# Sums of weights inside DRAM in halves and from the filter stage on, one split for the gates' four sums, and the last projection's first block loaded at another time

## The chip, the cores and the metric

The kernel runs on one core of a Trainium2 chip. The engines named here are PE (TensorE, the matrix products), DVE (VectorE), ACT (ScalarE), POOL (GpSimd) and SP (SyncE, which here only issues transfers); PEld is PE's loading of weights. The metric is device time in microseconds (us) of one execution. The kernel before was timed in three runs: 2376.48, 2383.24 and 2383.48 us, median 2383.24.

## The reference

One encoder layer on two sequences (`x_prompt` and `x_sample`) of 1024 rows and 1024 channels, all in 32-bit floats. After a norm, one projection makes everything else; a Fourier branch and a Hyena branch (two long convolutions with computed filters) are gated, projected, mixed and projected once more:

```python
xn = rmsnorm(x, g_pre)
p = xn @ w_in                      # fv, fg, hv (3 parts), hg, mg (2 parts): 8 x 1024 columns
fz = fftn(fv in 4 groups, axes=(sequence, group channel)).real
y_f = (fz * silu(fg)) @ w_fourier_out
v, x1, x2 = split(short_conv(hv, w_short), 3)
kf = hyena_filters(...)            # rfft of a two-sided filter, two orders
z = v
for n, gate in enumerate((x1, x2)):
    z = gate * long_conv(z, kf[:, n], hyena_d[n])
y_h = (z * silu(hg)) @ w_hyena_out
g_f, g_h = split(sigmoid(mg + b_merge), 2)
out = (g_f * y_f + g_h * y_h) @ w_out
return x + rmsnorm(out, g_post)
```

## The kernel before

Each 32-bit operand of a product is split into a rounded high part and the rest (`split`, L170 for the cast on ACT and L180 for the subtraction on DVE or POOL), and a product is three matmuls of high and low parts (`mm`, L193). So most groups of the profile bear the lines L170, L180 and L193, and go by their tiles' names. A `T`, `we`, `wh`, `wl` or `oT` is such a part; a subtraction `wl<-wr,wh` makes a low part.

The program runs through these stages:

1. *The start* (`phase_fourier`): 128-row blocks of the first sequence are loaded (L328), normed and transposed (`tpx`), the transposed rows are stored to DRAM (`d_x<-xg`, L362), and sums `eo` of them meet weights made from `w_fv` (`wfv` loads, L385; `wes`, `we`, `wo`) in the products `pfv`.
2. *The filter stage* (`phase_main`, about 230 to 650 us): 16 iterations make the filters' spectra (`kt`, stored to `d_k`) and between them project gates of the first sequence (`spill_gate`, product `pin`, weights `wr` loaded by SP, their low parts `wl` made on POOL).
3. *The branches* (`branches`, L1034 to L1105): for each step one `front(i)`, its gates, and the way back. Here `k<-d_k` loads bring the filter spectra, and the first sequence's weight parts go out to DRAM by transfers on POOL's queue (`d_w<-wh`, `d_w<-wl`, L858).
4. *The gates' projections of the second sequence* (`phase_tail`): products of 1024 x 1024 matrices cut in quarters, by Strassen and Winograd in seven products. One operand's seven blocks are B11, B21, B22 and the sums T1 to T4. The rows of the second sequence come back from DRAM (`xraw`, L1513) in four steps k; each step makes four sums of 512 elements and splits each of them into its tile T2, T3, T1 or T4 (eight operations). The other operand's sums are made by `prepare` (`wraw`, `wsum`, `s1` to `s4`). In the same stretch `last_sums` makes the sums of the last projection's weights `w_out`: loads `ws` (L1244), three subtractions on POOL, stores `d_t` (L1250).
5. *The nets*: 112 product steps of four projections (Fourier and Hyena output weights for two sequences), whose second operands are sums of weights that are read from DRAM (`wl<-d_s`, L1305). What is loaded and rounded when is written in a table of due steps: `at(98, load_own, ...)` has the step 98 issue a load. The rooms `x0{}` and `x1{}` and the four sum tiles are shared with the nets' own blocks.
6. *The last projection*: `prepare("o", ...)` for its rows (`wraw<-d_m`), blocks B11, B21 and B22 from `d_wo` (`load_own`, L1396, tiles `oB`), sums T1 to T4 from `d_t` (`load_sum`, L1402, tiles `oT`), each rounded in place by `round_z`. `first` opens it with products 11 (with B11) and 12 (with B21), then `part2` takes `s2` with T2, and so on.

The sums in `d_s` are made by transfers from DRAM to DRAM, some of which add to what is there (`accum_op=ADD`). `weight_sums` lists them: 11 for each of the two weights, 1 MB each, all on POOL's queue. Some read or add to what an earlier one wrote, and so wait for it, for example

```python
load(3, v[1, 0])
more(3, v[1, 1])
```

`front(i)` issues two of them for i = 2 to 12 (L1132 plain ones, L1133 adding ones). Eight copies of `w_out` by 512 KB to `d_wo` (L1524) are on SP's queue; they depend on nothing.

The order of the instructions on every engine isn't that of the text: a planner places the whole program by its own costs, and only `issue_after` and the dependences bind it. Queues issue in order: what stands behind a waiting instruction waits too.

Of the kernel before, what the change touches and what calls it, by code (L numbers as in the profile page):

```python
# [160 lines left out]
class K:  # L161
# [824 lines left out]
    def phase_main(self, nct=8, nb=NB, nf=16):  # L986
        tc, nc, a = self.tc, self.nc, self.a
        with ExitStack() as es:
# [25 lines left out]
            rates = self.filter_rates(1, 0, ws)  # L1014
            for i in range(nf):
                nxt = self.filter_taps((i + 1) % 2, (i + 1) // 2, rates, ws) if i + 1 < nf else None
# [14 lines left out]
            self.sums_due = list(self.weight_sums())  # L1031
            self.branches(nb, nct, ws)

    def branches(self, nb, nct, ws):  # L1034
# [13 lines left out]
        def front(i):  # L1048
            with tc.issue_after(self.pooled.ins):
                for f in self.sums_due[max(2 * i - 4, 0):max(2 * i - 2, 0)]:  # L1050
                    f()
            b, n, c = steps[i]
            src = self.conv(1, c, ws, "v", b) if n == 0 else Z.pop(c)
            return self.conv_front(src, ws)
# [69 lines left out]

    def weight_sums(self):

        nc, a = self.nc, self.a
        out = []
        for n, w in enumerate(("w_fo", "w_ho")):
            v = a[w].rearrange("(j i) p (h c) -> i h p j c", i=2, h=2)  # L1130
            d = self.d_s[n]
            load = lambda p, src, d=d: out.append(lambda: nc.gpsimd.dma_start(d[p], src))  # L1132
            more = lambda p, src, d=d: out.append(lambda: nc.gpsimd.dma_start(d[p], src, accum_op=ADD))  # L1133
# [10 lines left out]
            more(4, v[0, 1])  # L1144
        return out

    def phase_tail(self):
# [10 lines left out]
        with ExitStack() as es:  # L1158
# [96 lines left out]
            ROOM = ["T2", "T3", "T1", "T4"]  # L1255
# [26 lines left out]
            def block(g, i):  # L1282
# [8 lines left out]
                if i == 0:  # L1291
                    blocks[g] = gs.tile([P, 2, 4, 512], F32R, tag=ROOM[(g - 1) % 4], name="n", bufs=1)
# [106 lines left out]
            def load_sum(nm):  # L1399
                t = Z[nm] = gs.tile([P, 2, 4, 512], F32R, tag=nm, name=f"o{nm}", bufs=1)  # L1400
# [10 lines left out]
            for nm, room, t in (("B21", "x1{}", 88), ("B11", "x0{}", 98), ("B22", "x1{}", 110)):  # L1411
                at(t, load_own, nm, room)
            at(100, load_sum, "T4")
            at(104, load_sum, "T2")
            at(108, load_sum, "T3")
            for k in range(4):
                at(92 + k, round_z, "B21", k)
                at(100 + k, round_z, "B11", k)
            for k in range(2):
                at(103 + k, round_z, "T4", k)  # L1420
                at(107 + k, round_z, "T2", k)
# [87 lines left out]
            T = {j: gs.tile([P, 2, 4, 512], F32R, tag=j, name=j, bufs=1) for j in order}  # L1509
            for k in range(4):  # L1510
# [6 lines left out]
                for j, q in zip(order, (3, 1, 0, 2)):  # L1517
                    self.split(T[j][:, 0, k], T[j][:, 1, k], r[:, q], "dve", "act")
            pairs = lambda z: [(t[:, 0], t[:, 1]) for t in z]
            quad = lambda t: [(t[:, 0, k], t[:, 1, k]) for k in range(4)]  # L1520
            for j in order:
# [175 lines left out]
```

## Time and profile before

| | us |
|---|---|
| median of three runs | 2383.24 |
| the profiled execution | 2382.25 |
| its span | 2380.5 |
| PE busy | 2330.1 (98%) |
| DVE busy | 1973.3 (83%) |
| ACT busy | 1115.5 (47%) |
| POOL busy | 430.7 (18%) |
| mean granted clock of PE | 0.994 |

In a row of waits stand the engine, line and tile that waited, what released it, the total in us, how many times, and the longest. In a row of a timeline stand start and length in us, engine, line, operation, out<-in, shape, how many, and in brackets the idle time before it and its releaser; "SPq" is SP's queue of transfers. In a table of stretches stand the stretch and its length, busy us (and instructions) of PE, PEld, DVE, ACT and POOL, the granted clock of PE, the mean share of time in which the 16 DMA engines are busy, and GB/s. In a group of operations of one tile stand the least, median and greatest length in ns, and the first and last start. In a group of the page stand busy time, mean ns of one, and idle time before them with its releasers.

### The profile page before, as it was taken

The numbers are of one execution on the slowest core, as the hardware profiler recorded it, in microseconds if no ns is written. First come the engines' busy times: TensorE is split into PE (matmuls) and PEld (weight loads), VectorE is DVE, ScalarE is ACT, GpSimd is POOL, SyncE is SP. The second block draws the span as 40 slices with busy tenths as digits, with TensorE's granted clock in tenths as the row PEclk, the third lists the DMA queues.
The fourth block names the chain that finished last, engine by engine and source line by source line (L and its number), as shares of the span: only waits on it lengthen the run. The fifth ranks groups of instructions, "written<-read, shape, count | busy, mean of one in ns | idle before, by whom it ended". The sixth has DMA issues, their size and how long they took to land.

```text
span 2380.5 us, 36106 instructions
## 1 busy us (share of the span) xinstructions
PE 2330.1 (98%) x12796; PEld 2022.8 (85%) x12796; DVE 1973.3 (83%) x3416; ACT 1115.5 (47%) x2083; POOL 430.7 (18%) x406
## 2 busy tenths in 40 slices
PE   6999999999999999999999999999999999999998
PEld 5999888888888888888889888888788888888786
DVE  7775688878889999999889999997765578778987
ACT  6555667776753333334222332323444365557443
POOL 2342322222243333221000000111300000101211
PEclk9999999999999999999999999999999999999999
DMA  9646655555578787745444444445754688988644
GB/s 318 207 148 220 189 175 166 166 178 171 176 261 272 244 251 231 222 149 195 153 147 133 133 142 144 140 142 177 264 186 161 217 267 272 262 310 258 174 160 142
DMA packets 241888, 471.31 MB, mean 198 GB/s; under 512 B 24103, under 2 KB 81801, under 8 KB 241387
## 3 DMA queue, kind: packets, MB, share of 16 engines
q1 hardware_dynamic: 217949, 398.06, 51.0%
q0 software_dynamic: 23536, 70.91, 10.4%
q8 instruction: 101, 1.65, 0.3%
q14 instruction: 81, 0.66, 0.1%
q10 hardware_dynamic: 221, 0.04, 0.0%
HBM read 322.63 MB, written 173.54 MB: 208 GB/s over the span
## 4 chain that ended last, share of the span: by engine, by line
PE 52%; DVE 3%; DMA 3%; issue 1%; ACT 0%; SPq 0%; DVEq 0%; POOL 0%; POOLq 0%; ACTq 0%
PE pin L193 17%; PE pg L193 14%; PE pn L193 10%; PE pT L193 5%; PE pX L193 5%; DMA d_m<-gt 1%; PE tph L904 1%; DMA xraw<-d_x 1%; DMA d_sh<-x 0%; DVE gt L180 0%; DMA g<-d_g 0%; DVE T L180 0%; DVE wl L180 0%; DVE xraw L180 0%; DVE r L180 0%
## 5 line engine op out<-in xcount | busy, mean ns | idle before, releaser
L193 PE MATMUL pin<-x,wh 128*128 128x512 f32 x2880 | 909.8, 391 | 2.5 <-ACT ktmp L794 2.4
L193 PEld LDWEIGHTS pin<-x,wh 128*128 128x128 f32 x2880 | 534.3, 188 | 103.4 <-ACT ktmp L794 2.6
L193 PE MATMUL pin<-x,wl 128*128 128x512 f32 x1440 | 563.2, 391 | 0.0
L180 POOL TENSOR_TENSOR wl<-wr,wh 128x512 fp32r<-128x512 f32 x132 | 224.2, 1699 | 1104.5 <-ACT wh L170 668.6
L193 PEld LDWEIGHTS pin<-x,wl 128*128 128x128 f32 x1440 | 271.0, 188 | 50.8
L193 PE MATMUL pn<-n,wh 128*128 128x512 f32 x896 | 276.4, 389 | 0.1
L193 PEld LDWEIGHTS pn<-n,wh 128*128 128x128 f32 x896 | 168.1, 188 | 35.8 <-DVE n L180 0.5
L193 PE MATMUL pn<-n,wl 128*128 128x512 f32 x448 | 174.6, 390 | 1.6 <-DVE wl L180 1.5
L180 DVE TENSOR_TENSOR t<-pX,k 128x1024 f32<-128x1024 f32 x128 | 155.4, 1214 | 8.7 <-DMA k<-d_k 5.9
L193 PE MATMUL pX<-bh,cfwd 128*128 128x256 f32 x768 | 162.4, 288 | 0.0
L193 PE MATMUL pT<-cinv,yh 128*128 128x256 f32 x768 | 146.0, 284 | 0.3 <-DVE T0s L180 0.3
L170 ACT CAST wh<-wr 128x512 fp32r<-128x512 f32 x132 | 81.6, 618 | 132.2 <-PE pin L193 90.3
L170 ACT CAST bh<-b 128x512 fp32r<-128x512 f32 x144 | 88.4, 619 | 99.3 <-DVE b L180 73.7
L193 PEld LDWEIGHTS pX<-bh,cfwd 128*128 128x128 f32 x768 | 126.4, 190 | 3.1 <-DVE t L180 0.4
L193 PEld LDWEIGHTS pT<-cinv,yh 128*128 128x128 f32 x768 | 122.6, 190 | 6.6 <-ACT sg L1080 0.7
L170 ACT CAST yh<-y 128x512 fp32r<-128x512 f32 x96 | 59.6, 620 | 144.5 <-DVE y L180 144.4
L1344 POOL DMA_DIRECT2D d_m<-gt x32 | 27.5, 861 | 471.7 <-DVE gt L180 442.1
L193 PE MATMUL pT<-cinv,yl 128*128 128x256 f32 x384 | 109.1, 284 | 0.7 <-DVE yl L180 0.6
L193 PE MATMUL pX<-bl,cfwd 128*128 128x256 f32 x384 | 109.2, 284 | 0.4 <-DVE bl L180 0.4
L180 DVE TENSOR_TENSOR bl<-b,bh 128x512 fp32r<-128x512 f32 x144 | 101.5, 709 | 0.5 <-ACT bh L170 0.5
L193 PEld LDWEIGHTS pn<-n,wl 128*128 128x128 f32 x448 | 84.1, 188 | 19.7 <-DVE wl L180 2.5
L180 DVE TENSOR_TENSOR y<-t 128x512 f32<-128x512 f32 x128 | 91.8, 717 | 5.4 <-PE pT L193 4.9
(370 smaller groups left out, 5045.8 us busy)
## 6 DMA issues: line engine op xcount, KB each, us to landing
k<-d_k SPq DMA_DIRECT2D x128, 512.0 KB, 4.1
wr<-in_w_in SPq DMA_DIRECT2D x132, 256.0 KB, 3.4
d_g<-gt SPq DMA_DIRECT2D x124, 256.0 KB, 2.7
wl<-d_s SPq DMA_DIRECT2D x56, 512.0 KB, 5.8
d_k<-kt SPq DMA_DIRECT2D x128, 128.0 KB, 2.2
d_k<-kt SPq DMA_DIRECT2D x64, 256.0 KB, 2.4
g<-d_g SPq DMA_DIRECT2D x64, 256.0 KB, 5.5
r<-d_g SPq DMA_DIRECT2D x60, 256.0 KB, 5.7
```

The source lines that it names most:

```text
L170: self.rounded = nc.scalar.copy(h, src)
L180: return e.tensor_tensor(out, a, b, op=op)
L193: return self.nc.tensor.matmul(out, lhsT, rhs, start=start, stop=stop, skip_group_check=shared)
L904: nc.tensor.transpose(tp[:, q * P:(q + 1) * P], eo[:, e, q], self.ident)
L1344: nc.gpsimd.dma_start(dst, t, accum_op=ADD)
```

## The change

- `weight_sums` cuts each of its 22 transfers into two halves of 512 KB (over the row blocks j), 44 in all, and appends the eight copies to `d_wo`, which thereby go to POOL's queue. The list of 52 is `self.due`.
- `transfers(2)` issues two of them in each filter iteration from the second on (15 times) and then two in each front until the list is empty.
- The gates' opening has one tile `rooms` for the four sums, and each step k splits all four sums in one operation of 2048 elements on ACT and one on DVE. The nets' blocks and the last projection's sums use the four parts of `rooms` where they had tiles T1 to T4.
- In the last projection B11 is loaded at step 60 into `x1{}` and rounded at 64 to 67 (before: loaded at 98 into `x0{}`, rounded at 100 to 103); B21 is loaded at 98 into `x0{}` and rounded at 101 to 104 (before: 88 into `x1{}`, 92 to 95). The sums are loaded in the order T2, T3, T1 at steps 100, 104, 108 (before T4, T2, T3), T2 is rounded at 105 and 106 and T3 at 109 and 110; after `first`, T4 is loaded and T1 rounded, then the preparation is finished, B22 and T4 rounded.

```diff
@@ phase_main
+            self.due = self.weight_sums()
             for i in range(nf):
+                if i:
+                    self.transfers(2)
...
-            self.sums_due = list(self.weight_sums())
             self.branches(nb, nct, ws)
@@ branches
         def front(i):
-            with tc.issue_after(self.pooled.ins):
-                for f in self.sums_due[max(2 * i - 4, 0):max(2 * i - 2, 0)]:
-                    f()
+            if i < 16:
+                self.transfers(2)
@@
+    def transfers(self, n):
+        with self.tc.issue_after(self.pooled.ins):
+            for f in self.due[:n]:
+                f()
+        self.due = self.due[n:]
+
     def weight_sums(self):
...
+        def put(d, src, **how):
+            for j in (slice(0, 2), slice(2, 4)):
+                out.append(lambda j=j: nc.gpsimd.dma_start(d[:, j], src[:, j], **how))
...
-            load = lambda p, src, d=d: out.append(lambda: nc.gpsimd.dma_start(d[p], src))
-            more = lambda p, src, d=d: out.append(lambda: nc.gpsimd.dma_start(d[p], src, accum_op=ADD))
+            load = lambda p, src, d=d: put(d[p], src)
+            more = lambda p, src, d=d: put(d[p], src, accum_op=ADD)
...
+        for k in range(8):
+            out.append(lambda k=k: nc.gpsimd.dma_start(self.d_wo[k], a["w_out"][k * P:(k + 1) * P]))
         return out
@@ phase_tail
-            ROOM = ["T2", "T3", "T1", "T4"]
+            ROOM = [3, 1, 0, 2]
...
-                    blocks[g] = gs.tile([P, 2, 4, 512], F32R, tag=ROOM[(g - 1) % 4], name="n", bufs=1)
+                    blocks[g] = rooms[:, ROOM[(g - 1) % 4]]
...
-                t = Z[nm] = gs.tile([P, 2, 4, 512], F32R, tag=nm, name=f"o{nm}", bufs=1)
+                t = Z[nm] = rooms[:, {"T2": 2, "T3": 3, "T1": 1, "T4": 0}[nm]]
...
-            for nm, room, t in (("B21", "x1{}", 88), ("B11", "x0{}", 98), ("B22", "x1{}", 110)):
+            for nm, room, t in (("B11", "x1{}", 60), ("B21", "x0{}", 98), ("B22", "x1{}", 110)):
                 at(t, load_own, nm, room)
-            at(100, load_sum, "T4")
-            at(104, load_sum, "T2")
-            at(108, load_sum, "T3")
+            at(100, load_sum, "T2")
+            at(104, load_sum, "T3")
+            at(108, load_sum, "T1")
             for k in range(4):
-                at(92 + k, round_z, "B21", k)
-                at(100 + k, round_z, "B11", k)
+                at(64 + k, round_z, "B11", k)
+                at(101 + k, round_z, "B21", k)
             for k in range(2):
-                at(103 + k, round_z, "T4", k)
-                at(107 + k, round_z, "T2", k)
+                at(105 + k, round_z, "T2", k)
+                at(109 + k, round_z, "T3", k)
...
-            T = {j: gs.tile([P, 2, 4, 512], F32R, tag=j, name=j, bufs=1) for j in order}
+            rooms = gs.tile([P, 4, 2, 4, 512], F32R, name="rooms")
...
-                for j, q in zip(order, (3, 1, 0, 2)):
-                    self.split(T[j][:, 0, k], T[j][:, 1, k], r[:, q], "dve", "act")
+                self.split(rooms[:, :, 0, k], rooms[:, :, 1, k], r, "dve", "act")
...
-            for j in order:
-                Y[j] = quad(T[j])
-            for k in range(8):
-                nc.sync.dma_start(self.d_wo[k], a["w_out"][k * P:(k + 1) * P])
+            for j, q in zip(order, (3, 1, 0, 2)):
+                Y[j] = quad(rooms[:, q])
...
-            for k in range(2):
-                round_z("T3", k)
-            load_sum("T1")
             with tc.issue_after(self.copied.ins):
-                list(prep)
+                load_sum("T4")
                 for k in range(2):
                     round_z("T1", k)
+                list(prep)
                 for k in range(4):
                     round_z("B22", k)
-            Y["T1"] = quad(Z["T1"])
+                for k in range(2):
+                    round_z("T4", k)
+            Y["T4"] = quad(Z["T4"])
```

## The prediction

> **What bounds the kernel now.** I read the page's first part, then TensorE's (PE's) waits over the whole span, then a table of stretches around the places where those waits lie, and last the order in time at each place.
>
> ```profile
> span 2380.5 us, 36106 instructions
> PE 2330.1 (98%) x12796; PEld 2022.8 (85%) x12796; DVE 1973.3 (83%) x3416; ACT 1115.5 (47%) x2083; POOL 430.7 (18%) x406
> ```
>
> ```profile
> PE tpx L359 <- DVE x L344: 11.0, 1, 11.0
> PE pfv L193 <- ACT we L170: 4.5, 3, 2.3
> PE pg L193 <- ACT m L1215: 3.7, 1, 3.7
> PE pg L193 <- DVE wl L180: 3.4, 1, 3.4
> PE pX L193 <- DVE b L180: 2.2, 2, 1.8
> PE pn L193 <- DVE wl L180: 1.5, 1, 1.5
> PE pg L193 <- ACT gt L885: 1.2, 1, 1.2
> ```
>
> ```profile
> 0.00:50.00 50.00, 27.94 (x130) 22.16 (x131) 33.74 (x75) 34.01 (x57) 10.16 (x23) 0.90 0.96 334
> 240.00:640.00 400.00, 400.00 (x2195) 348.55 (x2194) 325.96 (x739) 276.60 (x592) 98.00 (x60) 1.00 0.55 173
> 690.00:970.00 280.00, 276.38 (x1625) 243.24 (x1625) 260.20 (x403) 99.47 (x178) 101.06 (x116) 1.00 0.82 255
> 1686.00:1706.00 20.00, 15.10 (x53) 11.57 (x52) 15.89 (x20) 6.82 (x13) 8.37 (x6) 0.83 0.97 346
> 2200.00:2225.00 25.00, 20.07 (x80) 15.57 (x79) 23.38 (x32) 14.55 (x21) 6.55 (x8) 0.93 0.99 267
> ```
>
> TensorE is the bound: 2330.1 of 2380.5 us. The change touches no matmul, so all that it can win lies in the 50.4 us in which PE is idle, and in stretches where a wait is followed by a lower granted clock (the column before the last two of the table: DMA share and GB/s close each row). The table places it: 22.06 us idle in the first 50, none in the filter stage, 3.62 in the first branches, 4.90 where the gates' projections open, 4.93 where the last projection opens. The clock costs about 50 x 0.10 = 5.0, 20 x 0.17 = 3.4 and 25 x 0.07 = 1.8 us more in the first, fourth and fifth of these stretches.
>
> **The change, part by part.**
>
> *The copies of the output weights leave the start.* Before, SP issues eight copies of 512 KB inside DRAM to `d_wo`:
>
> ```profile
> 8.78 5.67 SPq L1524 DMA_DIRECT2D d_wo<-in_w_out  x6
> 16.53 1.91 SPq L385 DMA_DIRECT2D wfv<-in_w_fv  x2
> 19.59 2.28 SPq L1524 DMA_DIRECT2D d_wo<-in_w_out  x2
> ```
>
> ```profile
> 30.35 0.52 PE L193 MATMUL pfv<-we,eh 128*128 128x260 f32 x2 [1.95 <-ACT we L170]
> 40.82 0.50 PE L193 MATMUL pfv<-we,eh 128*128 128x260 f32 x2 [2.35 <-ACT we L170]
> ```
>
> 4.19 MB at the stretch's 334 GB/s is 12.6 us of transfer time, and the issues hold SP for 7.95 us, ahead of the Fourier weights `wfv`. The DMA share is 0.96: the transfers compete. In the changed order SP goes from the x rows straight to `wfv`, and ACT and DVE prepare the next weights earlier. The two waits shown are 4.3 us, all waits for ACT's `we` 4.5; the clock lost after them is up to 5.0. Bounds: a gain of 9 (4.5 and nearly all of the clock's loss), and a loss of 2, since DVE is busy 33.74 of 50 us here and splitting a weight early delays an `eo` behind it. The 11.0 us at the very start stay: the x rows already stand ahead of the copies. I take **-5**: the two waits and a little of the clock.
>
> *Sums of weights halved and spread.* Before, 22 transfers of 1 MB go out in the branches, two per front, and one that reads what the last one wrote stands close behind it on POOL's queue:
>
> ```profile
> POOL d_s L1133 <- DMA d_s<-d_s: 20.6, 3, 13.5
> ```
>
> ```profile
> 935.91 1.21 POOL L1133 DMA_DIRECT2D d_s<-in_w_ho  x1 [13.48 <-DMA d_s<-d_s]
> ```
>
> ```profile
> 932.90 1.22 DVE L180 TENSOR_TENSOR t<-pX,k 128x1024 f32<-128x1024 f32 x1 [3.42 <-DMA k<-d_k]
> ```
>
> Behind the blocked POOL queue stand the low parts `wl` and the spills `d_w` of the input weights; beside it `k` loads come late, DVE waits, and the 1.8 us wait of `pX` for `b` follows. All PE idle time of these branches is 3.62 us: that is the upper bound of the gain. Afterwards there are 44 half transfers and the 8 copies. 30 go out in the filter stage, two in each of 15 iterations, 22 in the first 11 fronts; a transfer that depends on another is an iteration (15 of them fill the 400 us of the second row: 27 us each) or a front behind it, longer than the 13.5 us of the longest wait. POOL pays 30 issues more at up to the 1.21 us of the row quoted, 36 us on an engine that is 18% busy: nothing, as long as POOL's `wl` in the filter stage has room; POOL is busy 98 of 400 us there. I take **-3**.
>
> In the filter stage each pair moves 1 MB. The price from the rows: 22 such transfers raise the DMA share of the branches to 0.82; had it been 0.55 without them, each costs (0.82 - 0.55) x 280 / 22 = 3.4 us of DMA time. Fifteen pairs are 52 us in 400, share 0.55 to 0.68: still free. PE waits for nothing in these 400 us. A load behind a pair may come 3.4 us later. Bounds 0 and 15 x 3.4 = 51 us. I take **+1**, near the lower end, because the branches took whole megabytes at a higher share and lost 3.62 us over 22 of them, mostly to blocked queues.
>
> [...]
>
> *One split for four sums.* The gates' projections open with four row loads `xraw`; the last pair ends the waiting:
>
> ```profile
> 1686.23 1.03 SPq L1513 DMA_DIRECT2D xraw<-d_x  x2
> 1690.83 0.32 SPq L1250 DMA_DIRECT2D d_t<-ws  x1
> ```
>
> ```profile
> 1694.59 1.81 DVE L180 TENSOR_TENSOR xraw<-xraw 128x1024 f32<-128x1024 f32 x1 [0.63 <-DMA xraw<-d_x]
> 1696.43 1.65 DVE L176 SCALAR_TENSOR_TENSOR xraw<-xraw 128x512 f32<-128x512 f32 x1
> ```
>
> ```profile
> 1699.27 1.22 PE L193 MATMUL pg<-T,s2h 128*128 128x512 f32 x2 [3.70 <-ACT m L1215]
> 1704.13 0.63 PE L193 MATMUL pg<-T,s2l 128*128 128x512 f32 x1
> ```
>
> ```profile
> L170 ACT CAST T<-xraw x8: 613/622/628, 1681.2 to 1699.3; 128x512 fp32r<-128x512 f32 x8
> L180 DVE TENSOR_TENSOR T<-xraw,T x8: 677/681/1765, 1681.9 to 1701.0; 128x512 fp32r<-128x512 f32 x8
> ```
>
> ```profile
> L170 ACT CAST oT<-oT 128x1024 fp32r<-128x1024 f32 x8 | 8.2, 1042 | 0.8 <-DMA oT<-d_t 0.8
> L180 DVE TENSOR_TENSOR oT<-oT 128x1024 fp32r<-128x1024 f32 x8 | 9.7, 1217 | 0.0
> ```
>
> ```profile
> 1696.43 1.14 ACT L170 CAST T<-xraw 128x512 fp32r<-128x512 f32 x2 [6.64 <-DVE xraw L180]
> ```
>
> ```profile
> 27.32 1.30 DVE L180 TENSOR_TENSOR eo<-xg 128x512 f32<-128x512 f32 x2
> ```
>
> From 512 to 1024 elements a cast grows by 0.42 us, a subtraction by 0.54; so 2048 take 1.042 + 2 x 0.42 = 1.9 and 1.217 + 2 x 0.54 = 2.3 us. Two of 512 elements back to back take 1.14 and 1.30 us in all, so the second adds 0.52 and 0.62, and four cost 2.2 and 2.5: little is saved, but the first low part waits for the whole cast. In the changed order all `ws` loads and one `d_t` store (which waits for POOL, 1690.83 before) stand ahead of the fourth `xraw` pair: it goes out near 1691 instead of 1686.23. Its data then come some 1 to 2 us later (only that, as the older loads ahead of it fill the DMA either way), the sums end (1698.08, one addition of 0.68, and 1 to 2) at 1699.8 to 1700.8, the cast 1.9 later, the subtraction 2.3 later: 1704 to 1705, and the last product of `s2` that needs them ends about 0.6 behind. Before it ended at 1704.76. In return the copy `m`, which stood behind these casts and released PE at 1699.27, stands ahead of the last one: PE works off three of four `s2` steps early. The `gt` copies behind a 1.9 us cast cost the first `pg` 1.2 us or so, out of the same waiting time. Taken: **+0.5**, bounds -3 (the clock's 3.4 us mostly saved as the idle time falls into two pieces) and +3 (2 us later loads, and the clock falls all the same).
>
> [...]
>
> *The last projection's opening.*
>
> ```profile
> 2198.31 0.69 DVE L180 TENSOR_TENSOR wsum<-wraw 128x512 f32<-128x512 f32 x1 [5.50 <-DMA wraw<-d_m]
> 2207.92 0.68 DVE L180 TENSOR_TENSOR s2l<-wraw,s2h 128x512 fp32r<-128x512 f32 x1
> 2219.69 0.68 DVE L180 TENSOR_TENSOR wl<-wraw,wh 128x512 fp32r<-128x512 f32 x1
> ```
>
> ```profile
> 2220.43 0.50 PE L193 MATMUL pg<-oB,wl 128*128 128x512 f32 x1 [3.39 <-DVE wl L180]
> ```
>
> ```profile
> 2187.02 1.24 SPq L1175 DMA_DIRECT2D wraw<-d_m  x2
> 2191.31 2.18 SPq L1402 DMA_DIRECT2D oT<-d_t  x4
> ```
>
> The 3.39 us wait is for product 12's low weight, which DVE makes at 2219.69. From `s2l` to it DVE's order holds four `oT` subtractions of 1024 elements and nine operations of 512, 11.77 us with two short gaps; in the changed order two and eight are left. That takes away 2 x 1.217 + 0.68 = 3.1 us by durations, 2.8 by starts: ready at 2217.6 instead of 2220.4, where PE wants it at 2220.43 - 3.39 = 2217.0. The wait falls to about 0.6, and most of the clock's 1.8 comes back. The 1.5 us wait of `pn` for a `wl` goes as well, if the low weight stands ahead of `wsum`, as it does in the changed order, and is late by DVE's 5.50 us wait no more. B11's four rounds, 4 x 0.68 us of DVE, move to step 64, where no wait of PE shows. What is late next is `wsum`: before, SP had issued both halves of its `wraw` by 2188.3; now the second stands behind `T3`'s loads, which wait for PE to free the room, some 5 us later by my reading of the order. It lands near 2203 instead of 2198. Beyond 2205 it would hold the same low weight back. Bounds 0 and -6.7 (4.93 idle and 1.8 of clock); I take **-5**.
>
> **Sum:** -5 - 3 + 1 + 0.5 - 5 = -11.5 against the profiled execution, 2382.25 us (its span and 1.75 around it), which lies 1 us under the median of 2383.24: **2371 us**. The planner orders the whole program anew; that moves unrelated waits by some 3 us either way.
>
> **The rivals.**
>
> *A. The filter stage pays.* Transfers beside the tightest stretch: POOL issues two each iteration and loads behind them come late. For it: PE has no idle time there, DVE is busy 326 of 400 us, so a late `kt` or `wr` can't be caught up for free. Against it: DMA share 0.55, no PE wait. From 19 / 15 = 1.3 us an iteration on the kernel is slower than before by over 0.3%; with 2 us it is 2371 - 1 + 30 = 2400.
>
> *B. The start is bound by order, not by transfers.* Both waits are put down to ACT's `we`, and ACT is busy 34 and DVE 33.7 of those 50 us; then earlier data only move the waits to `eo`. Against it: a DMA share of 0.96. Gain 0: 2376.
>
> *C. The last projection only trades.* `wraw` lands after 2205, DVE waits as before at another place, and PE with it: 2371 + 5 = 2376; together with B 2381, no change.
>
> [...]
>
> **How the numbers follow.** Forecast with its own spread (2364 to 2374) 0.45; D 0.12; B alone 0.12, C alone 0.11, both 0.07; A 0.13, nearly all of it slower. A measurement of this kernel can tell about 0.3%, 7 us, from no change: under 2376.1 is faster. Forecast and D are faster, B and C alone half: 0.68. Same: the other half, both, and a little of A: 0.20. Slower: 0.12. For the range I go from 2359 (the bounds of start and last projection together) to 2385 (B and C, and a small A); A's far end and a little below are left out.
>
> **What would show it.** Right: no `d_wo` in the first 50 us and PE busy above 32 of them; POOL without a wait for `d_s`, and PE idle under 1 us from 690 to 970; PE at 400 of 400 in the filter stage; at the gates' opening two waits, for the cast and for the subtraction, of 5 to 6 us together; in the last opening no wait above 1 us for `wl`, the clock at 1.00. Wrong: PE waits for `wr`, `kt` or `b` between 240 and 640; first 50 us unchanged; a wait of DVE for `wraw` beyond 2205.

## The result and the profile after

The changed kernel takes 2393.44 us (median of six runs, 2391.0 to 2397.57) against 2381.88 for the kernel before (median of six, 2376.48 to 2384.98): a ratio of 1.0054, with a 95% interval of 1.0037 to 1.007. It is slower by some 11.6 us; 2371 was forecast. The profiled execution took 2393.43 us.

From the page of the kernel after, the span and the busy times, then PE's longest waits over the whole span:

```profile
span 2391.6 us, 36114 instructions
PE 2332.1 (98%) x12796; PEld 2026.4 (85%) x12796; DVE 1962.2 (82%) x3404; ACT 1116.9 (47%) x2075; POOL 496.4 (21%) x436
```

```profile
PE tpx L359 <- DVE x L344: 11.9, 1, 11.9
PE pXf L193 <- DVE kt L176: 5.0, 2, 3.6
PE pX L193 <- DVE t L180: 4.8, 2, 4.6
PE pXf L193 <- DVE b L180: 3.9, 1, 3.9
PE phd L295 <- DMA hd_w<-in_filt_w: 3.7, 1, 3.7
PE pg L193 <- ACT gt L885: 3.6, 1, 3.6
PE pfv L193 <- ACT eh L170: 3.6, 1, 3.6
PE tpx L193 <- DMA xk<-in_x1c: 2.3, 2, 1.7
PE pg L193 <- ACT u L1228: 1.9, 2, 1.5
```

PE's busy time grew by only 2.0 us; its idle time grew from 50.4 to 59.5. The waits for `we`, for `m` and the long one for `wl` are gone. Three of the largest are new (`pXf` for `kt`, `pXf` for `b`, `pX` for `t`), and none of these stands where the change was expected to win: they lie in the filter stage and the first steps of the branches. The table of stretches of the kernel after:

```profile
0.00:50.00 50.00, 28.94 (x167) 24.68 (x168) 38.18 (x83) 36.67 (x63) 16.25 (x26) 0.93 0.81 270
240.00:640.00 400.00, 394.04 (x2148) 342.23 (x2147) 325.53 (x731) 273.89 (x582) 133.16 (x85) 1.00 0.68 204
640.00:760.00 120.00, 108.78 (x583) 94.43 (x583) 84.94 (x168) 53.99 (x107) 40.12 (x45) 0.94 0.75 225
760.00:970.00 210.00, 209.79 (x1256) 186.33 (x1255) 204.03 (x320) 76.38 (x138) 82.71 (x86) 1.00 0.68 211
2205.00:2230.00 25.00, 24.03 (x106) 19.44 (x105) 17.41 (x24) 12.41 (x18) 5.34 (x7) 1.00 1.08 316
```

The filter stage, where PE had no idle time before, has 5.96 us of it; the stretch from 640 to 760 has 11.22, where the kernel before has 3.06:

```profile
640.00:760.00 120.00, 116.94 (x651) 101.58 (x651) 102.82 (x189) 54.07 (x106) 43.80 (x54) 1.00 0.78 258
```

Two traces that drift apart are hard to compare by the clock, so I lined them up by PE's work. Both kernels run 12,796 matmuls. For the n-th matmul of each, the start after minus the start before tells how far the changed kernel is behind by then. A flat stretch costs nothing, a step is time lost or won. (The order differs a little, so a single value is good to about 1 us.) Each row below is one n; the columns are its start in the kernel before and how far the changed kernel and five of the experiments are behind, in us. Negative is ahead.

```
 start before    changed   whole in     single      three    spaced,     single
                           fronts     halves      rooms col. last everywhere
         83.3      -5.46      -6.30      -6.20      -5.02      -5.97      -6.06
        182.1      -2.14      -4.13      -3.41      -1.43      -2.71      -2.34
        247.3      -2.12      -4.13      -3.38      -1.49      -2.71      -2.34
        359.6       5.21      -4.13      -3.38      -6.00      -2.71      -2.34
        612.4       7.07      -4.13      -2.77      -4.27      -2.71      -2.34
        688.4      12.97      -2.54       1.91      -2.23       0.03       2.58
        759.2      20.09      -3.21       6.32       2.96      -0.20       2.37
        925.3      18.70      -3.34       4.33       9.54      -2.17       0.40
        963.3      14.50      -4.44       0.13       5.47      -6.36      -3.79
       1675.8      14.90      -4.47       0.19      10.71      -5.66      -3.96
       1729.5      14.67      -2.56       0.70      10.85      -4.90      -3.41
       2183.6      14.29      -2.91       0.33      10.50      -4.78      -3.76
       2236.2      10.03      -7.72      -3.55       5.69      -9.72      -7.66
       2371.1      11.88      -5.82      -1.71       7.54      -7.88      -5.80
```

Read down the column of the changed kernel: 5.5 us won at the start, of which 3.3 are given back by 182; 9.2 lost between 247 and 612; 13.0 lost between 612 and 759; 1.4 won from there to 925 and 4.2 between 925 and 963; nothing at the gates' opening; 4.3 won and 1.9 lost in the last projection. So the wins are there, and 22 us are lost beside the weight transfers. (Each column is one execution of its kernel, and the times of one kernel differ by some us, as with the six from 2391.0 to 2397.57 above.)

What DVE waits for between 240 and 690 us in the kernel after (its two longest in total):

```profile
DVE kt L176 <- DMA d_k<-kt: 21.2, 7, 5.1
DVE kt L176 <- ACT ktmp L804: 19.2, 14, 3.1
```

The first row does not exist in the kernel before. `kt`, the filter's spectrum, has two rooms; SP stores each to `d_k`, and DVE can't write a room again before its store has landed. The times to landing of the `d_k` stores between 240 and 640 us, before and then after:

```profile
DMA to landing us min/median/max: 1.8/2.2/5.0
```

```profile
DMA to landing us min/median/max: 1.8/2.9/10.3
```

One place in full, from the kernel after: POOL issues a pair of halves at 673, DVE stands still for 5.07 us until a `d_k` store has landed, makes `b` late behind it, and PE idles 3.90 us.

```profile
673.14 1.41 POOL L1139 DMA_DIRECT2D d_s<-in_w_ho  x2
```

```profile
684.80 1.00 DVE L176 SCALAR_TENSOR_TENSOR kt<-pXf,th,ktmp 128x256 f32<-128x256 f32 x3 [5.07 <-DMA d_k<-kt]
```

```profile
690.57 1.19 PE L193 MATMUL pXf<-b,cfw 128*128 128x128 f32 x4 [3.90 <-DVE b L180]
```

Not every step goes that way. In the times of the kernel before, the 22.2 us fall in six steps: 1.7 near 296, 5.4 from 349 to 365, 1.9 at 491, 1.5 at 641, 4.4 from 677 to 688 and 7.4 from 717 to 721. Only the steps of 1.9 and 4.4 us follow a wait of DVE for a `d_k` store (4.13 and 5.07 us). At the step of 5.4 ACT waits for a load, `dec` (the filter's decay), that has one room. SP issued it at 339.57, behind its `wr` loads and just after a pair of POOL's at 339.07, and it landed 5.9 us later. ACT then works without a pause up to the `ktmp` that DVE and PE wait for:

```profile
345.50 0.42 ACT L733 ACTIVATE dec<-dec 128x256 f32<-128x256 f32 x1 [3.75 <-DMA dec<-in_filt_decay]
```

```profile
352.46 0.61 DVE L176 SCALAR_TENSOR_TENSOR kt<-pXf,th,ktmp 128x128 f32<-128x128 f32 x2 [3.14 <-ACT ktmp L804]
```

```profile
353.22 0.36 PE L193 MATMUL pXf<-bh,cfwd 128*128 128x256 f32 x1 [3.56 <-DVE kt L176]
```

The step of 1.5 us shows the same order of events, with a wait of 1.38 us for `dec`; the step of 1.7 was not followed back. At the step of 7.4 ACT waits for a weight load `wr`. SP had stood 7.5 us behind a `k` load that needs a `d_k` store; it then issued two `wr` loads, which landed after 10.1 and 10.7 us. ACT's `x` comes late by that, then DVE's `t`, then PE:

```profile
730.47 0.62 ACT L170 CAST wh<-wr 128x512 fp32r<-128x512 f32 x1 [13.79 <-DMA wr<-in_w_in]
```

```profile
734.70 0.55 PE L193 MATMUL pX<-bh,cfwd 128*128 128x256 f32 x1 [4.62 <-DVE t L180]
```

So late transfers of SP's queue reach PE by three routes: a `d_k` store over the two rooms of `kt`, the load `dec` over ACT, and `wr` behind a blocked queue, also over ACT. The lost time is more than the idle time, since the granted clock is 0.71 in the 5 us from 355 and 0.50 in those from 735.

### The profile page after: what moved, and what is told of

Read it like the earlier page. It is cut to its first block, busy times and chain, and to the rows that moved or that the text cites. A ratio compares the mean times of both kernels' runs of the same rounds, so it can differ in the third digit from the quotient of the medians.

```text
span 2391.6 us, 36114 instructions
## 1 busy us (share of the span) xinstructions
PE 2332.1 (98%) x12796; PEld 2026.4 (85%) x12796; DVE 1962.2 (82%) x3404; ACT 1116.9 (47%) x2075; POOL 496.4 (21%) x436
## 4 chain that ended last, share of the span: by engine, by line
PE 52%; DVE 2%; issue 2%; DMA 1%; ACT 1%; POOL 0%; SPq 0%; DVEq 0%; POOLq 0%; ACTq 0%
PE pin L193 18%; PE pg L193 14%; PE pn L193 10%; PE pT L193 5%; PE pX L193 5%; PE tph L904 1%; DMA xraw<-d_x 0%; DVE wl L180 0%; POOL d_m L1357 0%; DMA d_m<-gt 0%; ACT rooms L170 0%; DVE rooms L180 0%; DMA xr<-in_x 0%; DMA r<-d_g 0%; DVE o L176 0%
## 5 line engine op out<-in xcount | busy, mean ns | idle before, releaser
L180 POOL TENSOR_TENSOR wl<-wr,wh 128x512 fp32r<-128x512 f32 x132 | 253.6, 1921 | 1106.1 <-ACT wh L170 651.0
L193 PE MATMUL pn<-rooms,wh 128*128 128x512 f32 x864 | 266.2, 390 | 0.0
L193 PEld LDWEIGHTS pn<-rooms,wh 128*128 128x128 f32 x864 | 162.2, 188 | 33.5 <-DVE gt L180 0.2
L193 PE MATMUL pn<-rooms,wl 128*128 128x512 f32 x432 | 168.5, 390 | 1.0 <-DVE wl L180 1.0
L176 DVE SCALAR_TENSOR_TENSOR kt<-pXf,th,ktmp 128x128 f32<-128x128 f32 (+1 forms) x208 | 67.4, 372 | 45.1 <-DMA d_k<-kt 21.2
```

Source lines behind the costliest of these rows:

```text
L176: return self.nc.vector.scalar_tensor_tensor(out, a, s, b, op0=op0, op1=op1)
L180: return e.tensor_tensor(out, a, b, op=op)
L193: return self.nc.tensor.matmul(out, lhsT, rhs, start=start, stop=stop, skip_group_check=shared)
```

## The experiments

The theory (A): the bytes of the weight transfers beside the filter stage and the first fronts hold up the `d_k` stores; `kt`'s two rooms pass that on to DVE, and DVE to PE. Its rivals: halving itself costs (two issues instead of one); the planner's new order lost the time; any place for these transfers has the same price. Theory A names only the first of the three routes just shown. All edits are to the changed kernel unless said.

**The transfers as before, whole and in the fronts.**

```diff
-                if i:
-                    self.transfers(2)
...
-            if i < 16:
+            if 2 <= i < 17:
                 self.transfers(2)
...
-            for j in (slice(0, 2), slice(2, 4)):
-                out.append(lambda j=j: nc.gpsimd.dma_start(d[:, j], src[:, j], **how))
+            out.append(lambda: nc.gpsimd.dma_start(d, src, **how))
```

> The changed kernel with the sums of weights put back: 22 whole transfers, two per front from front 2 to 12, and the copies to d_wo in fronts 13 to 16. By PE's work the change lost 22 us between 290 and 730 us and won 4 between 930 and 960. Theory A (the transfers' bytes beside the filter stage and the first fronts hold up the stores of d_k and PE with them): the 22 go, the 4 come back as blocked POOL queue: 2393 - 22 + 4 = 2375, with PE at 400 of 400 us from 240 to 640. Rival (the planner's new order alone lost them): 2388 or more, with PE still idle in the filter stage.

Measured: 2378.43 us, ratio 0.9994 (0.9984 to 1.0005): no measurable difference from the kernel before, though its profiled execution, the fastest of its ten, ends 5.8 us ahead. PE loses nothing from 182 to 612 us. Without the weight transfers' new place the 22 us are gone. That supports A, but does not yet separate bytes from order, since the order changed with them.

**Halves, in the fronts alone.**

```diff
-                if i:
-                    self.transfers(2)
...
-            if i < 16:
+            if i < 26:
```

> The changed kernel with the 52 halves and copies in the fronts alone, two in each of fronts 0 to 25. Theory A: the filter stage is free again (7 to 9 us), what the first fronts lost (12 us between 640 and 730) stays at least in part, and the win at 930 to 960 stays: 2377 to 2386. Rival (halving itself costs): 2390 or more, the loss moved into the branches.

Measured: 2400.05 us, ratio 1.0087 (1.0071 to 1.0104). Outside the range and inside the rival's, but the trace gives another reason than the rival's. The filter stage is free (PE's work flat at -0.73 from 182 to 612); 7 us go between 647 and 688; 4 are won at 930 to 960. But 18.5 us go between 1100 and 1140. Eight copies and eight halves go out there in one burst, from 1087 to 1107; that they bunch because POOL has little other work to queue behind from front 16 on is likely, but was not tried. The burst begins:

```profile
1086.96 1.42 POOL L1137 DMA_DIRECT2D d_s<-in_w_ho  x2
1088.37 1.10 POOL L1137 DMA_DIRECT2D d_s<-d_s  x2
1089.46 1.94 POOL L1155 DMA_DIRECT2D d_wo<-in_w_out  x4
```

**Whole transfers at the same places.**

```diff
-                    self.transfers(2)
+                    self.transfers(1)
...
-            if i < 16:
+            if i < 7:
+                self.transfers(1)
+            elif i < 16:
                 self.transfers(2)
...
-            for j in (slice(0, 2), slice(2, 4)):
-                out.append(lambda j=j: nc.gpsimd.dma_start(d[:, j], src[:, j], **how))
+            out.append(lambda: nc.gpsimd.dma_start(d, src, **how))
```

> The changed kernel with whole transfers at the places of the pairs of halves, one per filter iteration and per front. The same bytes at the same places. Theory A (bytes): no change, 2390 to 2397. Rival (two issues and two fixed costs instead of one): 2380 to 2386.

Measured: 2391.09 us, ratio 1.0043 (1.0026 to 1.0059), which overlaps the changed kernel's. The order on ACT, DVE and SP is the changed kernel's but for a few places, and PE loses 7.3 us between 247 and 612 where the changed kernel lost 9.2. In these runs two halves issued together cost what one whole transfer costs, as far as can be told. That rival falls.

**Whole transfers in the second sequence's fronts, queued behind an ACT instruction.**

```diff
-            if i < 16:
-                self.transfers(2)
+            if i >= 16:
+                self.transfers(2, self.rounded)   # issue_after(self.rounded.ins), an ACT cast
```

> The changed kernel with whole transfers, two in each front of the second sequence (16 to 30, about 1000 to 1600 us), where the DMA share was 0.45 and PE had no idle time, and where POOL has no low parts to make. Theory A: the 22 us go and the win at 930 to 960 stays: 2367 to 2373. Rival (any place has its price): the loss moves there, 2380 or more.

Measured: 2439.23 us, ratio 1.025 (1.0233 to 1.0268). The edit didn't do what it was meant to: with an anchor on ACT, `issue_after` held back nothing on POOL, and the planner put the transfers at the start of the program:

```profile
2.59 3.74 POOL L1136 DMA_DIRECT2D d_s<-in_w_fo  x5
5.69 2.84 POOL L1136 DMA_DIRECT2D d_s<-in_w_ho  x3
```

PE is 51 us behind by 58 us and 65 behind by 107, and stays there to 700. As a measurement of the place it is void; it shows what the start pays for such transfers.

**Small transfers in their places.** 52 transfers of 1 KB into a room that nobody reads go where the halves went; the real ones are issued as in the run just told.

```diff
                 if i:
-                    self.transfers(2)
+                    self.dummies(2, 16, 16)
...
+            if i < 11:
+                self.dummies(2, 16, 16)
+            elif i >= 16:
+                self.transfers(2, self.rounded)
```

> The changed kernel with 52 transfers of 1 KB into a room that nobody reads in the places of the halves and copies, and the real transfers queued by POOL behind its last earlier work, wherever the planner then puts them. If they stay in the second sequence's fronts, the filter stage keeps POOL's issues and loses the bytes. Theory A (bytes): no PE idle time in the filter stage. Rival (POOL's issues and the new order): 4 us or more of PE idle time there, as in the changed kernel. If the planner puts the real transfers at the start, the start shows it by some 60 us and only the filter stage is to be read.

Measured: 2442.16 us, ratio 1.0257 (1.0242 to 1.0272), all of the loss at the start again. In the filter stage, to be read alone, PE's work is flat at 65.89 from 207 to 612 us: POOL's issues without the bytes cost nothing. The order is another than the changed kernel's, so this is one more draw for the order rival, and it lost nothing either.

**Twice the bytes.**

```diff
                     self.transfers(2)
+                    self.dummies(2, P, D)      # 2 x 512 KB more in each filter iteration
```

> The changed kernel with two further 512 KB transfers from DRAM to DRAM in each of the 15 filter iterations, into rooms that nobody reads. Theory A: the loss of 9 us between 290 and 640 us at least doubles, 2403 or more, and DVE's waits for d_k (21 us) grow with it. Rival (order, not bytes): within 4 us of the changed kernel's 2393.

Measured: 2394.68 us, ratio 1.0049 (1.0031 to 1.0067). The total missed: 2403 was expected. But PE's loss in the filter stage did what the theory says: 20.9 us between 247 and 612 (9.2 in the changed kernel) and 25.2 by 647. The total stays near because the changed kernel's 11.5 us between 647 and 759 did not come again: it loses nothing there. So this loss likely depends on where in the order the late store or load falls; the order is another here. DVE's waits for `d_k` hardly grew, against what I wrote: 22.6 us in seven waits between 240 and 690, where the changed kernel has 21.2 in seven. ACT's waits for `dec` grew there, from 9.1 to 14.3 us, and PE waits longest for ACT:

```profile
PE pXf L193 <- ACT kt L813: 5.3, 2, 4.5
```

So more bytes cost more, but not by way of `kt`'s rooms alone.

**One half at a time.** The two halves of a filter iteration go out half an iteration apart; the fronts are as in the changed kernel.

```diff
-                if i:
-                    self.transfers(2)
+                if i:
+                    self.transfers(1)
...
-                for sec, c in fill[...]:
-                    self.spill_gate(0, sec, c, ws)
+                for j, (sec, c) in enumerate(fill[...]):
+                    self.spill_gate(0, sec, c, ws)
+                    if i and not j:
+                        self.transfers(1)
```

> The changed kernel with the halves of the filter stage issued one at a time, half an iteration apart, not two together: the same bytes and the same count. Theory A says that a store waits behind what was issued just before it, so 512 KB at a time cost less than 1 MB: of the 9 us lost between 290 and 640 us at most 4 stay, 2386 to 2390. Rival (the mean DMA share decides): 2393 as the changed kernel.

Measured: 2381.38 us, ratio 1.0002 (0.9992 to 1.0011), better than the range expected. The stretch from 240 to 640 us and DVE's waits for `d_k` in it, of this kernel (in the changed kernel 16.1 us, six times):

```profile
240.00:640.00 400.00, 399.51 (x2199) 348.17 (x2198) 330.77 (x743) 279.06 (x597) 120.23 (x89) 1.00 0.71 211
```

```profile
DVE kt L176 <- DMA d_k<-kt: 3.0, 2, 2.6
```

The same bytes at an even higher DMA share (0.71 for 0.68) cost 0.6 us of PE's time instead of 9.2, so the mean share does not set the price. What goes out together does, or the moment at which it goes out: the edit changed both. (The latest `d_k` store still lands after 9.1 us, and ACT waits 12.5 us for `dec` between 240 and 690, more than in the changed kernel. So neither tells the loss alone; it depends on which of these waits reaches PE.) PE's matmuls stand in the changed kernel's order at 12,176 of 12,796 places, which leaves little to the rival of the order. What is left is lost after 647, where pairs go out.

**One half at a time in the first fronts too.**

```diff
             if i < 16:
-                self.transfers(2)
+                self.transfers(1 if i < 10 else 2)
```

> The kernel of the single halves with the fronts changed too: one half in each of fronts 0 to 9, then two. The single halves of the filter stage cost nothing between 290 and 640 us, but 9 us were lost between 640 and 760, where two went out at a time. Theory A: that loss falls to 4 us or less, the win at 930 to 960 stays: 2372 to 2378. Rival (beside the last d_k stores and the first k loads any transfer costs): 2380 to 2386.

Measured: 2375.65 us, ratio 0.9975 (0.9965 to 0.9985): faster than both kernels. Between 612 and 759 us it loses 4.7 us, a little over the 4 expected, all of it before 688; the part between 710 and 730 is gone, and the 4 us at 930 to 960 are won. What is left is no matter of pairs: with one half issued at 662 DVE stands 5.89 us for a `d_k` store until 674, and PE 4.39 us for `b`, about as long as in the changed kernel (3.90).

**Three rooms for `kt`.** The transfers stay as in the changed kernel; for the space, `T` and `x` get three rooms instead of four.

```diff
-            kt = ws.tile([P, 8, P], F32, tag="k", name="kt", bufs=2)
+            kt = ws.tile([P, 8, P], F32, tag="k", name="kt", bufs=3)
...
-        T = [ws.tile([P, 2, 2, 2, P], F32, tag="x", name=f"T{i}", bufs=4) for i in range(2)]
+        T = [ws.tile([P, 2, 2, 2, P], F32, tag="x", name=f"T{i}", bufs=3) for i in range(2)]
```

> The changed kernel with three rooms for kt (and for k) instead of two, so that DVE can go on while a store of d_k is late; for the space, the tiles T and x have three instead of four, which may bring waits of its own, seen as waits of ACT or DVE for T. Theory A (the two rooms pass the late store on to DVE and PE): DVE's waits for d_k between 240 and 690 us fall from 21 us to under 5 and the 9 us that PE lost between 290 and 640 to under 4. Rival (other loads or the new order pass it on): PE loses 7 us or more there.

Measured: 2384.65 us, ratio 1.001 (1.0 to 1.0019). The landing of the `d_k` stores and the stretch from 240 to 640 us, of this kernel:

```profile
DMA to landing us min/median/max: 1.8/3.1/12.3
```

```profile
240.00:640.00 400.00, 399.40 (x2217) 348.71 (x2217) 345.64 (x788) 277.47 (x597) 128.72 (x83) 1.00 0.70 212
```

The stores are as late as ever, and DVE waits for none of them; PE loses nothing between 247 and 612. So a third room ends DVE's waits for late stores. That these waits had cost the whole 9.2 us is not shown: the planner made another order (PE's matmuls keep their places at 6,637 of 12,796), ACT's waits for `dec` fell as well, from 9.1 to 1.8 us, and by the trace of the changed kernel only 1.9 of the 9.2 us go by way of the rooms. Between 612 and 759 this kernel still loses 7.2 us of the 13.0. (It loses 13 us from 688 to 1730, in the branches. The profiled execution was the slowest of its ten, 4.5 us above their median, so part of that is its own; that the rest is the price of `x`'s missing room is likely but was not tried.)

**Whole transfers spaced over the second sequence's fronts.** POOL copies one column of each front's input, and two transfers queue behind it; those in the filter stage and the first fronts are taken out. Three versions with the same order of instructions on every engine differ in one tile alone.

```diff
+            if i >= 16 and self.due:
+                seen = self.wp.tile([P, 1], F32, name="seen", tag="seen", bufs=1)
+                self.pooled = nc.gpsimd.tensor_copy(seen, src[:, 0:1])
+                self.transfers(2)
```

> The changed kernel with whole transfers, two in each front of the second sequence from front 16 on, held there by a one-column copy on POOL that reads the front's input. No such transfer stands beside the filter stage or the first sequence's branches, where POOL spills weights and SP stores d_k; the DMA share in their place was 0.45. Theory A (the stores of d_k come late beside these bytes, and DVE waits for kt's two buffers): 2393 - 22 = 2371, range 2367 to 2375, no wait of DVE's kt for d_k above 1 us in all, PE 400 of 400 us in the filter stage. Rival (the loss follows the transfers wherever they go): 2385 or more.

Measured: 2391.35 us, ratio 1.0045 (1.003 to 1.006). No wait for `d_k`, PE without idle time in the filter stage, and yet it falls behind by 0.6 us every 36 us there: its `pin` matmuls take 395 ns instead of 390. The column tile stands ahead of the tiles that hold the rows. In the next version it is 128 bytes wide:

> The kernel of the spaced whole transfers in the second sequence's fronts, with the one-column tile that POOL writes 128 bytes wide instead of 4; the order of the instructions is the same on every engine. In the 4-byte version pin matmuls took 395 ns instead of 390 and PE fell back by 0.6 us every 36 us without any idle time. Theory (the 4 bytes moved the tiles behind them to other addresses, and PE reads these more slowly): 390 ns again, no drift, 2391 - 13 = 2378 less what the spaced transfers win: 2370 to 2376. Rival (the transfers' new place or POOL's copies slow PE): 395 ns and 2388 to 2393 as before.

Measured: 2390.82 us, ratio 1.0033 (1.0021 to 1.0046), 394 ns: the expectation failed. This tile stands ahead of those with the rows as well. In the last version the 4-byte column comes from the pool that is opened last, behind all the others (in place of the line with `self.wp.tile`):

```diff
                     self.cin0 = mi.tile([P, 4 * P], F32, name="cin0")
+                    self.seen = mi.tile([P, 1], F32, name="seen")
```

> The kernel of the spaced whole transfers in the second sequence's fronts once more, same order on every engine, with POOL's one-column tile put behind all others instead of ahead of the rows' tiles. Theory (with the column ahead of them the rows' tiles had moved, by 128 bytes too, and pin matmuls took 394 to 395 ns for 390): 390 ns, no drift from 250 to 650 us, 2372 to 2378. Rival (the drift belongs to the order or to POOL's copies): 394 ns and 2388 or more.

Measured: 2373.31 us, ratio 0.9962 (0.995 to 0.9975): the fastest of all. The `pin` matmuls between 400 and 640 us in the kernel before, with the 128-byte column, and with the column last:

```profile
L193 PE MATMUL pin<-x,wh 128*128 128x512 f32 x501 | 157.3, 390 | 0.0
```

```profile
L193 PE MATMUL pin<-x,wh 128*128 128x512 f32 x497 | 158.2, 394 | 0.0
```

```profile
L193 PE MATMUL pin<-x,wh 128*128 128x512 f32 x501 | 157.4, 390 | 0.0
```

PE's work ends 7.9 us ahead of the kernel before. The branches have no idle time left, with a DMA share of 0.57 where it was 0.82 (the stretch of the kernel with the column last):

```profile
690.00:970.00 280.00, 280.00 (x1670) 248.82 (x1669) 263.22 (x423) 103.78 (x186) 96.04 (x96) 1.00 0.57 182
```

So the rival that every place has its price falls as well. The rival of the order falls with it: PE's matmuls stand in the changed kernel's order at 12,176 of 12,796 places here too.

**Four splits again at the gates' opening,** on the version with the 128-byte column, which is what it is compared with.

```diff
-                self.split(rooms[:, :, 0, k], rooms[:, :, 1, k], r, "dve", "act")
+                for q in (3, 1, 0, 2):
+                    self.split(rooms[:, q, 0, k], rooms[:, q, 1, k], r[:, q], "dve", "act")
```

> The kernel of the spaced whole transfers (128-byte column) with each step's four sums split in four operations again, as before the change, into the same tile. By the forecast the one split costs 0.5 us (-3 to 3) at the gates' opening: 2370 to 2376, and PE's work past 1730 us within 3 us of the kernel with one split. Rival (a large operation pays its fixed cost once): four splits lose about 1 us or more there.

Measured: 2387.66 us, ratio 1.0026 (1.0017 to 1.0035). The absolute time misses, because of the slow `pin` matmuls in both. Against the kernel it is compared with (2390.06 to 2391.68 us in five runs) all ten runs are lower, 2386.50 to 2389.28, so four splits are some 3 us faster. Only a part of that lies at the gates' opening: by PE's work between 1676 and 1730 us the one split loses 1.1 us and the four 0. That is in the forecast's bounds, and against the rival by which the large operation wins. The 1.1 us alone prove little, as other kernels with the one split lie between -0.3 and 1.9 us there.

## Why the prediction was wrong, step by step

**The sum failed above all at one term: "+1" for the pairs in the filter stage.** The changed kernel loses 22.2 us there and behind it: 9.2 between 247 and 612 us and 13.0 from there to 759. (The kernel with the column last, which has no such transfers there, loses 2.5 between 612 and 759; so the pairs' own price is nearer 20.) The price was set near the lower end because the mean DMA share would stay free, at 0.68. The share did come out at 0.68. But the mean did not tell how late a single transfer lands behind 1 MB: the `d_k` stores took up to 10.3 us where they had taken 5.0, and the `dec` loads up to 8.3 where they had taken 6.6. What should have been read is who waits for each landing there and how many rooms lie between: two for `kt`, one for `dec`. The term's bounds, 0 and 51 us, held the value; choosing near the lower end was the mistake. Rival A named the kind of loss ("a late `kt` or `wr`") but had a chance of 0.13. Its price of 1.3 to 2 us an iteration was too high for the filter stage (9.2 us in 15 iterations are 0.6 each); that its total comes out near the measured time is luck, since most of the loss lies at the first fronts, on which the sum put no price: there pairs go out while the last `d_k` stores are still under way, and `k` loads wait for these stores.

**Halves or whole transfers.** Whole and halved transfers at the same places took 2391.09 and 2393.44 us with overlapping intervals, and single halves (2381.38 us) beat both by 9.7 us or more: in this kernel the number of transfers did not show; the spacing did.

**The start, -5.** Right by 83 us (-5.5), then 3.3 of it given back: PE comes to the second half of the stage earlier than its `xk` loads do, and waits 2.3 us for them instead of 0.5. The waits for `we` went; PE waits 3.6 us for ACT's `eh` instead, which is rival B's mechanism in part. "PE busy above 32" of the first 50 us was wrong: 28.94. That a part would be given back was missing from the term, which came to -2.1 in place of -5.

**The branches, -3.** Right: 4.2 us won between 925 and 963, a little above the 3.62 that were called the upper bound, and POOL's waits for `d_s` down from about 50 us to 1.0. "PE idle under 1 us from 690 to 970" was wrong: it is 6.06, as part of the loss at the first fronts lies there too. This is the whole list of POOL's waits for `d_s` in the kernel after, from 640 to 980 us:

```profile
POOL d_s L1139 <- DMA d_s<-in_w_ho: 1.0, 1, 1.0
```

**The gates' opening, +0.5.** Right: -0.2. The one cast took 1.91 us and the subtraction 2.29 to 2.36 (1.9 and 2.3 forecast), the fourth pair of rows went out late, and two waits took the place of two:

```profile
1707.15 1.22 PE L193 MATMUL pg<-x,wh 128*128 128x512 f32 x2 [3.62 <-ACT gt L885]
1718.72 0.50 PE L193 MATMUL pg<-rooms,s2h 128*128 128x512 f32 x1 [0.84 <-DVE rooms L180]
```

The wait for the copies `gt` was longer than thought (3.62), that for the split shorter; together they are 4.46 us, where 5 to 6 were forecast. The one subtraction is shorter than the four were: four times 0.681 us (2.72) became 2.29, and four casts of 0.622 us (2.49) became 1.91. The chance D, 0.12 on a gain in time from the one large split, is not borne out: no run shows such a gain, and the run with four splits lost nothing at the opening (0 us, where the kernel it is compared with loses 1.1).

**The last projection, -5.** Right in its place: 4.9 us won between 2195 and 2227 in PE's work, the wait for product 12's low weight down from 3.39 to 0.68, the clock at 1.00. `wsum` did wait for the second half of `wraw`, 2.64 us until 2218.19; less the 14.3 us by which the kernel is behind, that is the 2203 or so that was forecast. A `wl` of the nets stands behind it, and PE waits 0.97 us for one at 2222.12. Then 2.5 us go again, 1.9 of them at two waits for the copies `u` (0.39 and 1.54), which the term left out:

```profile
2231.34 0.51 PE L193 MATMUL pg<-oB,wl 128*128 128x512 f32 x1 [0.68 <-DVE wl L180]
2239.78 0.73 PE L193 MATMUL pg<-rooms,s1h 128*128 128x512 f32 x2 [0.39 <-ACT u L1228]
2260.67 0.73 PE L193 MATMUL pg<-rooms,s1h 128*128 128x512 f32 x2 [1.54 <-ACT u L1228]
```

Put together by PE's work: -2.1, -4.2, -0.2, -2.4 and +22.2 make 13.3; with the 1.4 us won between 759 and 925 that is the 11.9 by which the trace ends behind. The four terms besides the pairs came to -8.9 where -12.5 was forecast, since the start and the last projection kept only about half of their 5 us each. Without the wrong term the forecast's direction would have held: with the transfers in the second sequence's fronts the kernel is faster by 0.4%.

**Left open:** why single halves make so many fewer landings late enough to matter, when the latest store lands about as late as before (9.1 and 10.3 us), and whether their size or their moment did it; how much of the loss each of the three routes would cost by itself, since no run closes one and leaves the others; and how much of the 13 us between 612 and 759 belongs to the order there, since the kernel with twice the bytes in the filter stage lost nothing from 647 on.

## What to carry to other kernels

Price a transfer that is moved by the stores and loads it will stand in front of, and count the rooms between their landing and the engine that bounds the stage; the mean DMA share gave no price here (9.2 us lost at 0.68, 0.6 at 0.71). Spreading the bytes singly helped here (2381.38 us, and 2375.65 with the first fronts too, against 2393.44), and putting them where nobody waits for a landing soon helped most (2373.31): the same bytes cost some 20 us in pairs beside stores and loads with one or two rooms, and 0.7 us by PE's work from 963 to 1676 beside the second sequence, where a single value is good to about 1 us. And line two traces up by the bound engine's work before explaining a sum: here it showed that one term of five turned a win into a loss. Then follow each step back to its own wait; the theory that explains one of them need not explain the largest.

## What the runs showed of the hardware

The same order of instructions, with a one-column tile allocated ahead of the rows' tiles or behind them, takes 2391.35 (4 bytes wide, ahead), 2390.82 (128 bytes wide, ahead) and 2373.31 us (4 bytes, behind). Between 400 and 640 us the `pin` matmuls take 395, 394 and 390 ns, with 0.0 us of idle time before them; the mean granted clocks of the three executions are 0.996, 0.996 and 0.998, 0.2% apart where the matmuls differ by 1.3%. Over all 4,320 of them the 4-byte version spends 20.1 us more than the kernel before (1493.1 and 1473.0); it is 18.0 us slower than the last version. POOL's copies of the column begin only after 1100 us, so they can't slow the matmuls of the filter stage. That the tiles' place in memory does it follows from the edit, as nothing else differs; the trace does not show the addresses, and which place is a good one was not tried.
